# A decoder layer on one core: three raw-weight tiles instead of two, two slots fewer, and four pieces of work issued at other times

## The chip, the cores and the metric

The kernel runs on one core of one Trainium2 chip. The core has a matrix engine (TensorE, PE in the rows; its weight loads are PEld), a vector engine (VectorE, DVE), a scalar engine (ScalarE, ACT), GpSimd (POOL) and a queue engine (SyncE, SP) that here issues the transfers between the chip's main memory and the core's on-chip memory. The metric is the time of one execution on the device, in microseconds (us); lower is better.

## The reference

One inference step of a one-layer decoder, in fp32, width 1024: two half feed-forward layers (FFN, inner width 2816) around a mixing layer of matrix-memory heads (mLSTM) and sliding-window attention (SWA), each between two RMS norms.

```python
def half_ffn(x, j, gpre, gpost):
    y = swiglu(rmsnorm(x, g[gpre]), ffn_w_gate[l, j], ffn_w_up[l, j], ffn_w_down[l, j])
    return x + 0.5 * rmsnorm(y, g[gpost])      # swiglu: (silu(x @ wg) * (x @ wu)) @ wd

x = half_ffn(x, 0, 0, 1)
h = rmsnorm(x, g[2])
...                                            # z = h @ w_in; mLSTM heads and SWA heads on z
u = jnp.concatenate([u_m, u_a], axis=-1)
x = x + rmsnorm(u @ w_out[l], g[3])
x = half_ffn(x, 1, 4, 5)
```

There are 1024 prompt tokens and 8 x 4 sample tokens, 1056 in all.

## The kernel before

**Tiling.** Activations lie with features on the 128 partitions and tokens along the free axis. The 1056 tokens are four quarters q of QW = 264 columns (256 of the prompt, 8 samples). The program has three phases: FFN 1 (phase 1), the mixing layer (phase 2), FFN 2 (phase 3). An fp32 product is made of three matmuls, wh·xh, wh·xl, wl·xh, where h and l are a rounded part and the rest (`mm3` and the loops of the FFN, all recorded at L158).

**Weights.** A raw block of weights, at most 128x1024 fp32 (512 KB), is loaded by SP into one of NRAW tiles called `raw` (`raw_tile`, L217; `prep`, L221). ScalarE casts it in pieces of 512 columns to `wh` and VectorE subtracts `wl = raw - wh` (`split`, L200 and L201). There are NW = 8 tiles each of `wh` and `wl`. A raw tile takes its next load when both have read it. `AHEAD = 3` units are asked for ahead of use.

**FFN.** First the inner activations: for each pair of 128 inner features, TensorE forms sums `gu` by a scheme of seven products from gate and up weights; ScalarE copies some of the sums out of their PSUM bank into `sc` (L957), the activations `h` go to main memory (`store_h`). Then the down projection `pd` in steps of quarters (STEPS): (0,1) and (2,3) in phase 1, (0,1), (2,), (3,) in phase 3. A step loads its `h` back (`load_h`, tiles `hq`, split by the same lines L200 and L201) and runs over 8 output blocks mo of 128 features; a block takes three raw loads (8, 8 and 6 rows of 128x128) and 66 matmuls for each quarter. `out_block` (L634 to L638) scales each result into `y` and sums its squares in `acc`, 528 columns wide: two halves, for the even and the odd mo.

**Norms.** `post` (L556) ends a quarter. `col_stats` adds the two halves of `acc` (VectorE, L248; not in phase 2, where both go to TensorE) and forms column sums `cs` by small matmuls; `rstd` takes the root on VectorE (some ten small instructions, L271 to L280), `row_bcast` spreads it over the partitions on TensorE (`rb`). Then `y*c + x` is formed with `x` loaded back, again with squares and a second `col_stats` for the norm of the next phase. Quarters 0 to 2 of phase 3 end in `store_y` (L1046): transposes of y into a bank `yT` on TensorE, copies `yo` on ScalarE (L1058) or VectorE (L1060), and stores by SP. Quarter 3, the last, is done by the class `Last` (L646), which transposes x and y ahead and block by block.

**What sets the order.** The program is written in the order of a clock `od.now`, TensorE's time as the program estimates it. `od.spawn(generator, delay)` starts side work at a due time, each `yield` moves it on by so many us, and `od.tick` between matmuls lets what is due be written. PQ gives the delay with which `post` starts for each phase and quarter, PW and PL the delays inside it. The tile framework then fixes each engine's order and puts in the waits. All tiles of 528 fp32 columns (x, y, h, hq, sums of activations) come from one pool of NSLOT = 66 slots. PSUM banks of 512 columns are in four groups: 3 "mm", 2 "a", 2 "b", 1 "c" (the statistics).

Of the kernel before, what the change touches and what calls it, by code (L numbers as in the profile page):

```python
# [16 lines left out]
P = 128  # L17
# [6 lines left out]
QW = 264  # L24
# [4 lines left out]
NSLOT, NW, NRAW, NTMP = 66, 8, 2, 8  # L29
# [8 lines left out]
PQ = {1: [4.0, 8.0, 0, 8.0], 2: [2.0, 8.0, 0, 6.0], 3: [0] * 4}  # L38
# [113 lines left out]
def pe(K, out, lhsT, rhs, start=True, stop=True, tr=False, **kw):  # L152
    n = int(np.prod(rhs.shape[1:]))
    if tr:
        K.nc.tensor.transpose(out, lhsT, rhs)
        K.od.now += 0.11
        return
    K.nc.tensor.matmul(out, lhsT, rhs, start=start, stop=stop, **kw)  # L158
    if rhs.dtype == F32R:
        K.od.now += 0.0025 + (n if n >= 213 else 256) / 2400  # L160
    else:
        K.od.now += (4 if rhs.dtype == F32 else 1) * max(n, 64) / 2400
# [79 lines left out]
def col_stats(K, acc, phase):  # L242

    ps = sbank(K, "cs")
    n = 2
    if phase != 2:

        K.nc.vector.tensor_tensor(acc[:, 0:QW], acc[:, 0:QW], acc[:, QW:2 * QW], op=ALU.add)  # L248
        n = 1
    for j, w in enumerate(WIN):  # L250
        for i in range(n):
            pe(K, ps[:, j:j + 1], acc[:, i * QW + w:i * QW + w + P], K.ones, start=(i == 0), stop=(i == n - 1))
    return ps[:, 0:3]
# [302 lines left out]
def post(K, phase, q, y, acc, half, nxt, gpre=None):  # L556

    nc = K.nc
    x = []
    for kp in range(4):  # L560
        t = slot(K, "x")
        nc.sync.dma_start(t, K.xs[q][kp])
        if phase == 1 and q == 0:

            nc.vector.tensor_tensor(pair(t), pair(t), K.r[q].unsqueeze(1).to_broadcast([P, 2, QW]), op=ALU.mult)
        x.append(t)
    yield PW[0]
    ss = col_stats(K, acc.pop(), phase)

    c = rstd(K, ss, 4.0 / D, 4.0 * EPS) if half else rstd(K, ss)  # L570
    yield PW[1]
# [5 lines left out]
    for kp in range(4):  # L577
# [19 lines left out]
        yield PW[2] if q > 1 else PL[phase]  # L597
# [4 lines left out]
    K.od.done.add(("x", phase, q))  # L602
    yield PW[3]
    r = rstd(K, col_stats(K, acc, phase))
# [36 lines left out]
class Last:  # L641
# [30 lines left out]
    def block(self, mo, ps):  # L672
# [16 lines left out]
        if mo == 3:  # L689
            K.od.spawn(self.first(self.t), 3.0)  # L690
        elif mo > 3:
            K.od.spawn(self.second(mo, y), 3.0)
# [197 lines left out]
def ffn(K, phase, j, gpost, nxt, gpre=None):  # L890
# [94 lines left out]
    for si, step in enumerate(steps):  # L985
# [3 lines left out]
        for mo in range(KT):  # L989
# [3 lines left out]
            for q in step:  # L993
                ps[q] = bank(K, "pd", "mm" if last else ("mm", "a", "mm", "b", "mm", "a", "b")[npd % 7])[:, 0:QW]
                npd += 1
# [50 lines left out]
def store_y(K, q, y):  # L1046
    nc = K.nc
    for j in range(3):
        w = P if j < 2 else 8
        for x in range(2):  # L1050
            ps = bank(K, "yT")
# [960 lines left out]
```

## Time and profile before

| | |
|---|---|
| time of three runs | 2021.26 us median (2019.25, 2021.26, 2025.99) |
| profiled execution | 2024.76 us, of which the span of the profile is 2023.0 us |
| instructions in the span | 40250 |
| TensorE | 1982.2 us busy, 98% of the span |
| VectorE, ScalarE | 1168.0 us (58%), 874.9 us (43%) |
| DMA | 216.68 MB, 107 GB/s over the span |
| phase 1: gu, pd | 73 to 483 us, 483 to 749 us |
| phase 3: gu, pd | 1316 to 1726 us, 1726 to 2015 us |

The profile is of one execution, so its stretches add to 2023.0 us; the three runs are other executions of the same program. TensorE is busy nearly everywhere, so what can be had without fewer matmuls is the time in which it waits, and the time in which its clock is not granted in full.

### The profile page before, as it was taken

What the parts mean: (1) busy time and instruction counts of PE and PEld (TensorE: products, weight loads), DVE (VectorE), ACT (ScalarE), POOL (GpSimd) and SP (SyncE); (2) the same over time, 40 slices, a digit from 0 to 9 for tenths busy, and PEclk for the clock granted to TensorE, in tenths of its full rate; (3) what the DMA queues carried; (4) which work ended last, traced back from release to release, by engine and by line L of the source; (5) the groups of instructions that cost most, each with busy time, mean ns of one, the idle gap of its engine ahead of it and who ended that gap; (6) DMA issues with size and microseconds to landing.
All of it is one profiled execution on the core that took longest, in us unless ns stands there. A gap on an engine that the chain in (4) does not pass through costs nothing.

```text
span 2023.0 us, 40250 instructions
## 1 busy us (share of the span) xinstructions
PE 1982.2 (98%) x16108; PEld 1939.7 (96%) x16108; DVE 1168.0 (58%) x2801; ACT 874.9 (43%) x2097; POOL 40.2 (2%) x191
## 2 busy tenths in 40 slices
PE   7999999999999999999999999999999999999997
PEld 6999999999999999987998999999999999999997
DVE  7755555557248336467456758875555556434663
ACT  6533333336346332356253655443333334434553
POOL 1000000000000003000001000000000000000000
PEclk9999999999999999999999999999999999999999
DMA  6223222235356252201324143222223224545773
GB/s 219 70 75 97 74 74 75 87 100 170 95 161 203 89 140 93 53 1 39 97 53 136 43 137 113 107 85 74 75 74 96 74 75 132 155 124 164 223 217 116
DMA packets 281725, 216.68 MB, mean 107 GB/s; under 512 B 21097, under 2 KB 254689, under 8 KB 281537
## 3 DMA queue, kind: packets, MB, share of 16 engines
q1 hardware_dynamic: 281536, 214.11, 35.1%
q8 instruction: 126, 2.06, 0.4%
q14 instruction: 63, 0.51, 0.1%
HBM read 171.38 MB, written 42.49 MB: 106 GB/s over the span
## 4 chain that ended last, share of the span: by engine, by line
PE 87%; DVE 5%; DMA 5%; ACT 2%; issue 1%; SPq 0%; DVEq 0%; ACTq 0%
PE gu L158 40%; PE pd L158 21%; PE pz L158 6%; PE pw L158 4%; PE pl L158 3%; PE pv L158 3%; DMA raw<-ffn_w_down 2%; PE po L158 2%; PE cs L158 1%; DVE wl L201 1%; PE sws L158 1%; PE swo L158 1%; DMA hq<-h 1%; PE E L158 1%; ACT wh L200 1%
## 5 line engine op out<-in xcount | busy, mean ns | idle before, releaser
L158 PE MATMUL gu<-Xl,wh 128*128 128x264 f32 x2240 | 637.4, 285 | 0.0
L158 PE MATMUL gu<-Xh,wh 128*128 128x264 f32 x2240 | 636.6, 284 | 0.3 <-ACT sc L957 0.2
L158 PE MATMUL gu<-Xh,wl 128*128 128x264 f32 x2240 | 635.7, 284 | 0.0
L158 PE MATMUL pd<-hq,wh 128*128 128x264 f32 x2816 | 522.6, 286 | 1.1 <-ACT yo L1058 1.1
L201 DVE TENSOR_TENSOR wl<-raw,wh 128x512 fp32r<-128x512 f32 x450 | 295.9, 668 | 385.0 <-ACT wh L200 379.7
L200 ACT CAST wh<-raw 128x512 fp32r<-128x512 f32 x450 | 265.1, 601 | 457.0 <-PE pd L158 185.7
L158 PEld LDWEIGHTS pd<-hq,wh 128*128 128x128 f32 x2816 | 439.3, 189 | 1.4 <-ACT yo L1058 1.3
L158 PEld LDWEIGHTS gu<-Xh,wl 128*128 128x128 f32 x2240 | 422.3, 189 | 0.0
L158 PEld LDWEIGHTS gu<-Xh,wh 128*128 128x128 f32 x2240 | 421.5, 188 | 0.8 <-ACT sc L957 0.7
L158 PEld LDWEIGHTS gu<-Xl,wh 128*128 128x128 f32 x2240 | 420.8, 188 | 0.0
L158 PE MATMUL pd<-hq,wl 128*128 128x264 f32 x1408 | 402.0, 285 | 0.0
L158 PEld LDWEIGHTS pd<-hq,wl 128*128 128x128 f32 x1408 | 265.9, 189 | 0.0
L957 ACT COPY sc<-gu 128x264 f32<-128x264 f32 x240 | 90.8, 379 | 275.9 <-PE gu L158 273.8
L201 DVE TENSOR_TENSOR wl<-ws,wh 128x512 fp32r<-128x512 f32 x160 | 108.8, 690 | 86.3 <-ACT wh L200 83.3
L968 DVE TENSOR_TENSOR h<-gu,sc 128x264 f32<-128x264 f32 x120 | 51.8, 432 | 105.6 <-PE gu L158 85.4
L158 PE MATMUL pz<-xh,wh 128*128 128x264 f32 x352 | 102.9, 292 | 0.9 <-DVE z L1887 0.9
L158 PE MATMUL pz<-xh,wl 128*128 128x264 f32 x352 | 101.8, 289 | 0.0
L158 PE MATMUL pz<-xl,wh 128*128 128x264 f32 x352 | 101.3, 288 | 0.0
L969 ACT ACTIVATE h<-h 128x264 f32<-128x264 f32 x120 | 50.9, 425 | 106.7 <-DVE h L968 106.7
L200 ACT CAST wh<-ws 128x512 fp32r<-128x512 f32 x160 | 95.8, 623 | 1.5 <-DVE ws L771 1.5
L974 DVE TENSOR_TENSOR sc<-gu,sc 128x264 f32<-128x264 f32 x120 | 51.7, 432 | 56.7 <-PE gu L158 50.9
L158 PE MATMUL pw<-uh,wh 128*128 128x264 f32 x256 | 74.1, 290 | 0.0
(405 smaller groups left out, 2971.2 us busy)
## 6 DMA issues: line engine op xcount, KB each, us to landing
raw<-ffn_w_down SPq DMA_DIRECT2D x80, 512.0 KB
raw<-ffn_w_gate SPq DMA_DIRECT2D x42, 512.0 KB
raw<-ffn_w_up SPq DMA_DIRECT2D x42, 512.0 KB
h<-h SPq DMA_DIRECT2D x80, 264.0 KB
hq<-h SPq DMA_DIRECT2D x160, 132.0 KB
raw<-ffn_w_down SPq DMA_DIRECT2D x40, 384.0 KB
x<-xs SPq DMA_DIRECT2D x48, 264.0 KB
raw<-w_in SPq DMA_DIRECT2D x21, 512.0 KB
```

What stands on the lines that cost most here:

```text
L158: K.nc.tensor.matmul(out, lhsT, rhs, start=start, stop=stop, **kw)
L200: K.nc.scalar.copy(hi, src)
L201: (eng or K.nc.vector).tensor_tensor(lo, src, hi.bitcast(F32), op=ALU.subtract)
L957: nc.scalar.copy(sc[n][:, g], ps)
L968: nc.vector.tensor_tensor(d, bk[tg, g], sc[n][:, g], op=ALU.add)
L969: nc.scalar.activation(d, d, AF.Silu)
L974: nc.vector.tensor_tensor(sc[n][:, g], src, sc[n][:, g], op=ALU.add)
```

## The change

- NRAW goes from 2 to 3: a third raw tile; a load waits for the reads of the third block before it instead of the second. NSLOT goes from 66 to 64.
- The addition of the two halves is taken out of `col_stats` into a new function `halves`, which `post` calls first of all for the first norm, and ahead of the wait PW[3] for the second: 4 and 6 us of `od.now` ahead of the matmuls that read the sum, where it stood right before them.
- In `post`, the four loads of x are issued together; the multiplication of x by its row factor, which only quarter 0 of phase 1 has, moves behind `rstd`.
- In phase 3, `post` starts 3, 7 and 3 us after its step for quarters 0, 1 and 2 (PQ, before 0); quarter 2 steps by PL = 4 us and not PW[2] = 1; the transposes of the first half of the last quarter's y start 5 us after block 3, not 3.
- Banks: the step (2,) of phase 3 takes "mm" for all its `pd` results, as the last step did; `store_y` takes "a" and "b" in turn for quarters 0 and 1 and "b" for quarter 2, where it took "mm".

```diff
--- before.py
+++ after.py
@@ -26,7 +26,7 @@
 
 WIN = [0, 128, 136]
 STEPS = {1: [(0, 1), (2, 3)], 2: [(0, 1), (2, 3)], 3: [(0, 1), (2,), (3,)]}
-NSLOT, NW, NRAW, NTMP = 66, 8, 2, 8
+NSLOT, NW, NRAW, NTMP = 64, 8, 3, 8
 BANKS = dict(mm=3, a=2, b=2, c=1)
 AHEAD = 3
 
@@ -35,7 +35,7 @@
 HW = 0.6
 
 NHELD, NS = 5, 2
-PQ = {1: [4.0, 8.0, 0, 8.0], 2: [2.0, 8.0, 0, 6.0], 3: [0] * 4}
+PQ = {1: [4.0, 8.0, 0, 8.0], 2: [2.0, 8.0, 0, 6.0], 3: [3.0, 7.0, 3.0, 0]}
 XQ = [0, 3.0, 10.0, 20.0]
 PL = {1: 4.0, 2: 2.5, 3: 4.0}
 NP = [1.6, 3.0]
@@ -239,17 +239,20 @@
         K.od.tick()
 
 
-def col_stats(K, acc, phase):
+def halves(K, acc, phase):
+
+    if phase == 2:
+        return [acc[:, 0:QW], acc[:, QW:2 * QW]]
+    K.nc.vector.tensor_tensor(acc[:, 0:QW], acc[:, 0:QW], acc[:, QW:2 * QW], op=ALU.add)
+    return [acc[:, 0:QW]]
+
+
+def col_stats(K, sq):
 
     ps = sbank(K, "cs")
-    n = 2
-    if phase != 2:
-
-        K.nc.vector.tensor_tensor(acc[:, 0:QW], acc[:, 0:QW], acc[:, QW:2 * QW], op=ALU.add)
-        n = 1
     for j, w in enumerate(WIN):
-        for i in range(n):
-            pe(K, ps[:, j:j + 1], acc[:, i * QW + w:i * QW + w + P], K.ones, start=(i == 0), stop=(i == n - 1))
+        for i, s in enumerate(sq):
+            pe(K, ps[:, j:j + 1], s[:, w:w + P], K.ones, start=(i == 0), stop=(i == len(sq) - 1))
     return ps[:, 0:3]
 
 
@@ -556,18 +559,18 @@
 def post(K, phase, q, y, acc, half, nxt, gpre=None):
 
     nc = K.nc
-    x = []
+    sq = halves(K, acc.pop(), phase)
+    x = [slot(K, "x") for _ in range(4)]
     for kp in range(4):
-        t = slot(K, "x")
-        nc.sync.dma_start(t, K.xs[q][kp])
-        if phase == 1 and q == 0:
-
+        nc.sync.dma_start(x[kp], K.xs[q][kp])
+    yield PW[0]
+    ss = col_stats(K, sq)
+
+    c = rstd(K, ss, 4.0 / D, 4.0 * EPS) if half else rstd(K, ss)
+    if phase == 1 and q == 0:
+
+        for t in x:
             nc.vector.tensor_tensor(pair(t), pair(t), K.r[q].unsqueeze(1).to_broadcast([P, 2, QW]), op=ALU.mult)
-        x.append(t)
-    yield PW[0]
-    ss = col_stats(K, acc.pop(), phase)
-
-    c = rstd(K, ss, 4.0 / D, 4.0 * EPS) if half else rstd(K, ss)
     yield PW[1]
     cr = tmp(K, "cr", QW)
     nc.scalar.copy(cr, row_bcast(K, c))
@@ -594,14 +597,15 @@
                 hi, lo = [t[k][g][:, i * QW:(i + 1) * QW] for t in (K.xh, K.xl)]
                 nc.scalar.activation(hi, y[kp][:, s], AF.Copy, scale=gk)
                 nc.vector.scalar_tensor_tensor(lo, y[kp][:, s], gk, hi.bitcast(F32), op0=ALU.mult, op1=ALU.subtract)
-        yield PW[2] if q > 1 else PL[phase]
+        yield PW[2] if q > 1 and phase < 3 else PL[phase]
     if not nxt:
         yield 2.0
         yield from store_y(K, q, y)
         return
     K.od.done.add(("x", phase, q))
+    sq = halves(K, acc, phase)
     yield PW[3]
-    r = rstd(K, col_stats(K, acc, phase))
+    r = rstd(K, col_stats(K, sq))
     yield PW[4]
     if nxt == "mix":
         rc = K.kp.tile([P, 3], F32, tag=f"rc{q}", name=nm(K, "rc"), bufs=1)
@@ -687,7 +691,7 @@
         if mo == 6:
             K.od.spawn(self.stats(0), 2.0)
         if mo == 3:
-            K.od.spawn(self.first(self.t), 3.0)
+            K.od.spawn(self.first(self.t), 5.0)
         elif mo > 3:
             K.od.spawn(self.second(mo, y), 3.0)
 
@@ -991,7 +995,7 @@
                 od.spawn(load_h(K, hs, steps[si + 1]))
             ps = {}
             for q in step:
-                ps[q] = bank(K, "pd", "mm" if last else ("mm", "a", "mm", "b", "mm", "a", "b")[npd % 7])[:, 0:QW]
+                ps[q] = bank(K, "pd", "mm" if len(step) == 1 else ("mm", "a", "mm", "b", "mm", "a", "b")[npd % 7])[:, 0:QW]
                 npd += 1
             for a in range(0, MT, 8):
                 for x, (dh, dl) in enumerate(od.take()):
@@ -1048,7 +1052,7 @@
     for j in range(3):
         w = P if j < 2 else 8
         for x in range(2):
-            ps = bank(K, "yT")
+            ps = bank(K, "yT", "ab"[x] if q < 2 else "b")
             for i in range(4):
                 k = 4 * x + i
                 o = (k % 2) * QW + j * P
```

How the rows of three queues stand before and after, in the order of the program (a name ends in the number of its tile; line numbers behind L158 differ by four between the two programs):

**VectorE, end of step (0,1) of phase 1.** `sq_6408` and `sq_6412` are the squares of quarters 0 and 1, `x` the four loads for quarter 0. Before:

```order
L638 TENSOR_TENSOR sq_6408<-sq_6408,sq_7604 128x528
L565 TENSOR_TENSOR x_7829<-x_7829,rrow_355 128x528
L638 TENSOR_TENSOR sq_6412<-sq_6412,sq_7608 128x528
L201 TENSOR_TENSOR wl_7786<-raw_7783,wh_7785 128x512
L201 TENSOR_TENSOR wl_7790<-raw_7783,wh_7789 128x512
L565 TENSOR_TENSOR x_7832<-x_7832,rrow_355 128x528
L565 TENSOR_TENSOR x_7835<-x_7835,rrow_355 128x528
L565 TENSOR_TENSOR x_7838<-x_7838,rrow_355 128x528
L248 TENSOR_TENSOR sq_6408<-sq_6408 128x264
L201 TENSOR_TENSOR wl_7856<-raw_7853,wh_7855 128x512
L201 TENSOR_TENSOR wl_7860<-raw_7853,wh_7859 128x512
L248 TENSOR_TENSOR sq_6412<-sq_6412 128x264
```

With the change:

```order
L642 TENSOR_TENSOR sq_6408<-sq_6408,sq_7604 128x528
L642 TENSOR_TENSOR sq_6412<-sq_6412,sq_7608 128x528
L201 TENSOR_TENSOR wl_7786<-raw_7783,wh_7785 128x512
L201 TENSOR_TENSOR wl_7790<-raw_7783,wh_7789 128x512
L246 TENSOR_TENSOR sq_6408<-sq_6408 128x264
L201 TENSOR_TENSOR wl_7853<-raw_7850,wh_7852 128x512
L246 TENSOR_TENSOR sq_6412<-sq_6412 128x264
L573 TENSOR_TENSOR x_7830<-x_7830,rrow_355 128x528
L201 TENSOR_TENSOR wl_7857<-raw_7850,wh_7856 128x512
L573 TENSOR_TENSOR x_7831<-x_7831,rrow_355 128x528
L573 TENSOR_TENSOR x_7832<-x_7832,rrow_355 128x528
L573 TENSOR_TENSOR x_7833<-x_7833,rrow_355 128x528
```

The halves of quarter 0 (L248, now L246) are added ahead of the multiplications of x by `rrow`, and those of quarter 1 one row later; all four multiplications stand behind them.

**ScalarE, the change from gu to pd in phase 3.** `hq_...` are activations loaded back, `wh_21569` and `wh_21573` the casts of the first block of down weights, `sc_21605` the copies of the last sums for which TensorE's next `gu` products need the bank. Before:

```order
L200 CAST hq_21517<-hq_21517 128x264
L200 CAST hq_21527<-hq_21527 128x264
L957 COPY sc_21605<-gu_21311 128x264
L200 CAST hq_21531<-hq_21531 128x264
L200 CAST hq_21542<-hq_21542 128x264
L200 CAST hq_21546<-hq_21546 128x264
L957 COPY sc_21605<-gu_21342 128x264
L200 CAST hq_21556<-hq_21556 128x264
L200 CAST hq_21560<-hq_21560 128x264
L200 CAST wh_21569<-raw_21567 128x512
L200 CAST wh_21573<-raw_21567 128x512
```

With the change:

```order
L200 CAST hq_21477<-hq_21477 128x264
L200 CAST wh_21569<-raw_21567 128x512
L200 CAST hq_21481<-hq_21481 128x264
L200 CAST hq_21491<-hq_21491 128x264
L200 CAST hq_21495<-hq_21495 128x264
L200 CAST wh_21573<-raw_21567 128x512
L200 CAST hq_21513<-hq_21513 128x264
L200 CAST hq_21517<-hq_21517 128x264
L200 CAST hq_21527<-hq_21527 128x264
L961 COPY sc_21605<-gu_21311 128x264
L200 CAST hq_21531<-hq_21531 128x264
L961 COPY sc_21605<-gu_21342 128x264
```

The casts of the first down block come ahead of the copies of `sc_21605`; before, they came behind them. SP issues that block's load ahead of the forty `hq` loads, and before it stood among them (behind `hq_21560`); every `hq` load that waits for a slot waits for the matmul for which, before, the second load behind it waited. On TensorE, 12 of the pd matmuls stand among the last 50 gu matmuls. The same rows stand in phase 1.

**SP, end of step (2,) of phase 3.** The raw blocks are those of mo 6 (its third) and mo 7; `o_y` are output stores, `hq` the activations of quarter 3. Before:

```order
L225 DMA raw_23957<-ffn_w_down 128x6x128
L1038 DMA hq_23970<-h_18630 128x264
L1038 DMA hq_23980<-h_18634 128x264
L1038 DMA hq_23990<-h_19116 128x264
L225 DMA raw_24001<-ffn_w_down 128x8x128
L1038 DMA hq_24014<-h_19120 128x264
L1038 DMA hq_24024<-h_19602 128x264
L1038 DMA hq_24034<-h_19606 128x264
L1038 DMA hq_24044<-h_20088 128x264
L225 DMA raw_24051<-ffn_w_down 128x8x128
L1038 DMA hq_24064<-h_20092 128x264
```

With the change:

```order
L225 DMA raw_23961<-ffn_w_down 128x6x128
L1069 DMA o_y_sample<-yo_23797 8x512
L1069 DMA o_y_prompt<-yo_23805 128x512
L1042 DMA hq_23854<-h_16664 128x264
L1069 DMA o_y_sample<-yo_23825 8x512
L1069 DMA o_y_prompt<-yo_23833 128x512
...
L1042 DMA hq_23947<-h_18148 128x264
L1042 DMA hq_23957<-h_18630 128x264
L1042 DMA hq_23977<-h_18634 128x264
L1042 DMA hq_23987<-h_19116 128x264
L1042 DMA hq_23997<-h_19120 128x264
L225 DMA raw_24005<-ffn_w_down 128x8x128
```

Between the last block of mo 6 and the first of mo 7 stand now 18 transfers (6 of them stores, 12 `hq`; eight rows are left out), before 3.

On TensorE, the matmuls `cs` of the second norm stand 6 rows earlier in phase 1 for quarter 0 and 68 rows earlier for quarter 2, which falls in the mixing layer; the `cs` of phase 2's step (0,1) three rows later. The FFN's gate and up loads now have the third block's load ahead of the `store_h` stores; that load waits for a VectorE instruction which comes before those for which the stores wait.

## Rows read from the trace of the kernel before

**Rows 1.** The page of the profile: the span, the engines' busy time (share of the span in brackets, instructions after the x), and the chain of work that ended last.

```profile
span 2023.0 us, 40250 instructions
...
PE 1982.2 (98%) x16108; PEld 1939.7 (96%) x16108; DVE 1168.0 (58%) x2801; ACT 874.9 (43%) x2097; POOL 40.2 (2%) x191
...
PE 87%; DVE 5%; DMA 5%; ACT 2%; issue 1%; SPq 0%; DVEq 0%; ACTq 0%
```

**Rows 2.** Everything that the matmuls of TensorE waited for over the whole span, by line and releaser: us in total, times, the longest (rows of start-up and of small waits left out).

```profile
PE cs L158 <- DVE sq L248: 3.2, 3, 1.7
PE yT L155 <- ACT yo L1058: 2.7, 1, 2.7
...
PE yT L155 <- ACT y L686: 2.2, 2, 1.9
...
PE cs L158 <- DVE sq L587: 1.3, 1, 1.3
...
PE pd L158 <- ACT yo L1058: 1.1, 1, 1.1
PE pz L158 <- DVE z L1887: 0.9, 1, 0.9
...
PE yT L155 <- DVE y L579: 0.8, 1, 0.8
...
PE cs L158 <- DVE sq L638: 0.6, 1, 0.6
...
PE gu L158 <- ACT sc L957: 0.2, 1, 0.2
```

**Rows 3.** VectorE's instructions in order of time about 620 us (start, busy us, line, operation, out and in, count): the end of the first half of phase 1's down projection.

```profile
619.42 1.29 DVE L201 TENSOR_TENSOR wl<-raw,wh 128x512 fp32r<-128x512 f32 x2
620.63 1.94 DVE L565 TENSOR_TENSOR x<-x,rrow 128x528 f32<-128x528 f32 x3
622.48 0.43 DVE L248 TENSOR_TENSOR sq<-sq 128x264 f32<-128x264 f32 x1
```

**Rows 4.** Stretches of 2 us at four places where TensorE had waited: busy time and instructions of PE, PEld, DVE, ACT and POOL, then PEclk, the granted clock of TensorE as a share of full speed, DMA share and GB/s.

```profile
623.00:625.00 2.00, 1.94 (x14) 1.97 (x15) 1.86 (x5) 0.60 (x2) 0.00 (x0) 0.87 0.97 324
625.00:627.00 2.00, 2.00 (x11) 2.00 (x10) 1.15 (x8) 0.44 (x1) 0.00 (x0) 0.50 0.78 216
627.00:629.00 2.00, 2.00 (x15) 2.00 (x15) 0.91 (x2) 0.58 (x2) 0.00 (x0) 0.78 0.30 88
...
786.00:788.00 2.00, 2.00 (x11) 2.00 (x11) 0.97 (x5) 0.00 (x0) 0.19 (x1) 0.50 0.86 266
...
1894.00:1896.00 2.00, 2.00 (x12) 2.00 (x11) 1.48 (x3) 0.95 (x2) 0.00 (x0) 0.56 0.94 281
1896.00:1898.00 2.00, 2.00 (x12) 2.00 (x12) 1.00 (x2) 1.93 (x5) 0.00 (x0) 0.59 0.98 299
...
1938.00:1940.00 2.00, 1.98 (x16) 1.98 (x17) 0.41 (x1) 1.06 (x2) 0.00 (x0) 1.00 0.99 347
```

**Rows 5.** Stretches of 10 us in the two last steps of phase 3, with the columns of rows 4.

```profile
1886.00:1896.00 10.00, 7.32 (x55) 7.08 (x55) 5.20 (x9) 5.13 (x10) 0.00 (x0) 0.91 0.63 188
...
1936.00:1946.00 10.00, 9.00 (x75) 8.79 (x74) 6.10 (x18) 3.86 (x10) 0.00 (x0) 1.00 0.72 224
1946.00:1956.00 10.00, 8.84 (x74) 8.39 (x73) 9.19 (x16) 5.83 (x14) 0.00 (x0) 1.00 0.57 166
1956.00:1966.00 10.00, 9.75 (x82) 9.11 (x80) 4.59 (x9) 4.92 (x10) 0.00 (x0) 1.00 0.73 215
1966.00:1976.00 10.00, 9.06 (x74) 9.06 (x75) 4.30 (x8) 4.46 (x11) 0.00 (x0) 1.00 0.62 183
1976.00:1986.00 10.00, 7.57 (x62) 7.12 (x62) 4.65 (x8) 6.10 (x13) 0.00 (x0) 1.00 0.50 148
```

**Rows 6.** The chain that ended last, of 1926 to 1992 us alone: its shares by line, and one of its eight transfers.

```profile
by line: DMA raw<-ffn_w_down 53.5%; PE pd L158 11.4%; issue 10.3%; ACT wh L200 9.1%; DVE wl L201 8.9%; DVE y L579 1.5%; PE yT L155 1.5%; DVE yo L1060 1.0%; DVE y L578 0.9%; ACT yT L712 0.7%; ACT hq L200 0.5%; ACT y L634 0.4%; ACTq L200 0.3%
...
1927.92 4.61 DMA raw<-ffn_w_down
```

**Rows 7.** All casts of raw down-projection weights on ScalarE, 1926 to 1992 us: duration in ns (least, median, most), the first and the last start, forms.

```profile
L200 ACT CAST wh<-raw x42: 400/618/623, 1926.2 to 1991.4; 128x512 fp32r<-128x512 f32 x35, 128x256 fp32r<-128x256 f32 x7
```

**Rows 8.** The subtractions that follow those casts on VectorE, and all DMA traffic of 1926 to 1990 us.

```profile
L201 DVE TENSOR_TENSOR wl<-raw,wh 128x512 fp32r<-128x512 f32 (+1 forms) x40 | 24.3, 642 | 28.3 <-ACT wh L200 26.5 <-PE pd L158 1.3
...
DMA packets 20942, 12.97 MB, mean 203 GB/s; under 512 B 528, under 2 KB 19385, under 8 KB 20937
```

**Rows 9.** TensorE's gu matmuls of 1714 us, in order of time (between the two rows shown stand 45 others, one matmul each).

```profile
1713.77 0.28 PE L158 MATMUL gu<-Xh,wh 128*128 128x264 f32 x1
...
1719.40 0.29 PE L158 MATMUL gu<-Xl,wh 128*128 128x264 f32 x1
```

**Rows 10.** ScalarE about the first change from gu to pd, the DMA issues of SP about the second (SPq; the duration is that of the whole run of issues), and ScalarE there.

```profile
475.93 0.79 ACT L200 CAST hq<-hq 128x264 fp32r<-128x264 f32 x2 [0.16 <-DMA hq<-h]
476.63 0.37 ACT L957 COPY sc<-gu 128x264 f32<-128x264 f32 x1
...
1706.16 12.94 SPq L1038 DMA_DIRECT2D hq<-h  x26
...
1718.99 1.10 ACT L200 CAST hq<-hq 128x264 fp32r<-128x264 f32 x3 [0.82 <-DMA hq<-h]
1720.00 0.37 ACT L957 COPY sc<-gu 128x264 f32<-128x264 f32 x1
```

## The prediction

> **What bounds the kernel now.** I read the page first. TensorE is busy 98% of 2023.0 us and 87% of the chain that ended last is TensorE [rows 1]; the change takes no matmul away, so it can only win back waits of TensorE and stretches in which its clock is not granted in full. Second view: what its matmuls waited for [rows 2]. The sums `cs` wait for the addition of the halves (L248) three times, 3.2 us in all; other waits hang on transposed outputs (`yo`, `y`). The gu stretches, where most of the work lies, wait 0.2 us.
>
> Third view: the granted clock after a wait. From 623 to 629 us it was 0.87, 0.50 and 0.78 in three stretches of 2 us, at 1894 us 0.56 and 0.59 [rows 4]. The missing shares times 2 us give 0.85 x 2 = 1.7 us at both places; 0.50 of full speed is the lower of the two levels. It fell to 0.50 behind the wait of 783 us too, but stayed at 1.00 behind that of 1937 us [rows 4]. So a wait costs its length, and sometimes 1.7 us on top.
>
> Last view: the two last steps of phase 3. From 1936 to 1986 us TensorE was busy 9.00 + 8.84 + 9.75 + 9.06 + 7.57 = 44.2 of 50 us, from 1886 to 1896 us 7.32 of 10 [rows 5]. In this stretch the chain is not TensorE's: 53.5% are loads of raw down weights, 11.4% pd matmuls [rows 6]. The 42 casts of 1926.2 to 1991.4 us belong to 21 blocks [rows 7], 65.2/20.5 = 3.2 us a block, 9.5 us for the three of an output block. TensorE needs less: 46 matmuls took 5.63 us, 0.122 us each [rows 9], so 66 take 8.1 us, with the eight transposes of a block, at the same pitch, 9.0. Raw supply, with two tiles, bounds it here.
>
> **The change part by part.**
>
> *Third raw tile, end of phase 3.* A tile's cycle is two of the intervals, 6.4 us: a load (4.6 us in the one shown [rows 6]), two casts at 0.62 us [rows 7], the last subtraction (0.64 us, [rows 8]), some of it overlapped. With three tiles the same cycle gives a block every 2.1 us and 6.4 us per output block, under the 8.1 to 9 that TensorE needs. The cover of the loads is then TensorE itself. The lost time is 50 - 44.2 = 5.8 us after 1936 us and 2.7 us at 1890 us, with 1.7 us of clock behind it. The 2.7 us wait is for `yo` [rows 2]: copies that stand on ScalarE behind a cast whose block is late. With the supply ahead and `store_y` on banks of its own, I expect all of it back: 10.2 us. Not all may come: the transposes of the last quarter share one "b" bank pair with `store_y` and need an eviction between neighbours (512 columns, as the cast's 0.62 us [rows 7]), and 18 transfers now stand ahead of the first block of mo 7. At 0.50 us an issue (12.94/26, [rows 10]) these are 9 us, against two output blocks (16 us) before the block is needed. The bound is from 0 to 3.5 us (a wait of 1.8 and a clock fall of 1.7); I take 0.8, nearest to single evictions.
>
> *Halves earlier.* At 621 us `cs` waits 1.7 us, the longest of its three [rows 2], as VectorE works three multiplications (1.94 us) and then the addition, 622.48 to 622.91 [rows 3]. Now the addition stands right behind the subtraction that ends at 620.71, so it is ready about 621.1, and TensorE asked 1.7 us ahead of 622.91, at 621.2 or a little later. Back come 1.7 us and the clock's 1.7: 3.4 us. The other two share 3.2 - 1.7 = 1.5 us. That of 1937 us is the 1.0 missing in the first of the five stretches [rows 5] and already in the 5.8; that of 656 us, 0.5, goes likewise: 0.5. The added instructions are none; the multiplications moved behind `rstd` are VectorE work beside pd matmuls.
>
> *Quarter 2's second norm, in the mixing layer.* Its `cs` stand 68 rows earlier on TensorE, so the pieces that crowd the wait `pz <- z` (0.9 us, [rows 2]) spread out. That wait may go or stay, and with it the clock: 0 to 0.9 + 1.7 = 2.6 us. I take most of the wait, 0.7, and half of the clock's 1.7, since behind another wait of about this length, that of 1937 us, it did not fall [rows 4]: 1.6.
>
> *Phase 2's step.* `cs` is asked three matmuls later, 0.4 of the 0.6 us [rows 2]. The wait for L587 (1.3 us) stays.
>
> *Two slots fewer, and the down block's load ahead.* At each change from gu to pd, `hq` loads take slots that gu matmuls free, and each now waits for the matmul of the second load behind it: two loads at 0.50 us [rows 10], 1.0 us later. ScalarE, which was waiting for those loads (0.82 us), also casts the first down block there, two casts, before the copy of `sc`; 1.24 - 0.82 = 0.4 us more, partly overlapped, say 0.2. Queued behind are the copies at 1720.00 and 476.63 us [rows 10], for which gu needs the bank. In phase 3 TensorE already waited 0.2 us for this copy [rows 2], so the delay shows: 1.1 us after one pd matmul that is moved into it. In phase 1 it did not, so some 0.4 us is cover: 0.7. Together 1.8 us lost, bounds 0 and 1.8 + 2 x 1.7 = 5.2 if the clock falls both times. The pd matmuls moved among gu cost nothing of their own.
>
> *Issued later, and nothing else.* The later start of `post` in phase 3, its slower pace for quarter 2 and the later transposes of the last quarter move small matmuls and transposes to other places among pd matmuls of the same steps, with the same count; their cover is the 64.5 us of a step (8 x 66 x 0.122 [rows 9]). If it were gone, by running past the end of step (2,), each pair of `yT` would be a wait of about 0.62 us in the last step; that is in the 3.5 above. The stores that `store_y` issues move with it and are the 18 transfers counted there. The four x loads of a `post` are issued in one piece, 4 x 0.50 us of SP's queue [rows 10], with a raw block ahead of them where there was one behind: no pd wait for `wh` or `wl` appears among TensorE's waits [rows 2], so that is hidden by blocks already split. In gu the third block is issued ahead of the `h` stores but waits for an earlier VectorE instruction than they do; that VectorE work hides it. Bounds: the gu wait of 0.2 us from below, and see the third rival.
>
> Sum: 10.2 - 0.8 + 3.4 + 0.5 + 1.6 + 0.4 - 1.8 = **13.5 us** shorter. Against the profiled execution's 2024.76 us that is 2011.3; that execution lies 3.5 us above the median of the runs, 2021.26, so the runs should come at about **2008 us**.
>
> **A rule against it.** The loads of 1926 to 1990 us moved 203 GB/s [rows 8], while stretches of 2 us reached 347 GB/s at a DMA share of 0.99 [rows 4]; so there is room. The Trainium skill, "DMA: Bandwidth & Descriptors", § Issuing engines are not separate DMA queues, states that all transfers run on the same 16 DMA engines and interleave there, so another one in flight adds no bandwidth of itself. By that rule alone a third load only stretches the other two; it is the first rival, and the trace agrees with it only where the share is near 0.99.
>
> **Rivals.**
>
> *1. The loads share, and supply stays the bound.* If a load in flight with two others takes 3/2 of its time, a block still comes every 3.2 us and the 5.8 us stay lost; the wait of 1890 us too. Against it speak shares of 0.50 to 0.73 over the 50 us [rows 5]; for it, the 18 transfers in one run and the stretches near 0.99. Then 13.5 - 9.4 = 4.1 us remain: about 2017 us.
>
> *2. The halves come no earlier in time.* If VectorE is behind when `halves` is due, the waits at 621, 656 and 1937 us stay with the clock's fall: 3.4 + 0.5 + 1.0, and the mixing layer's 1.6 with them, 6.5 us less: about 2014 us. For it: VectorE runs without a break before 622 us [rows 3]. Against it: its order has the addition ahead of what delayed it.
>
> *3. Slower: SP's queue in gu.* SP issues in order. If the third block's load, now ahead of four `h` stores, waits at the queue's head, the stores are late, and slots, two fewer, come free late for the next pair's `h`. This would come with each pair of inner blocks that stores, 10 in each FFN, 20 in all; from 13.5/20 = 0.7 us a pair on it eats the whole gain, and at 1.1 us a pair it ends 8.5 us slower, about 2030 us. Against it speaks the order of the waits; for it, that ScalarE's copies already touch TensorE there (0.2 us).
>
> **How the numbers follow.** Forecast 0.66 (2004 to 2012 us: with every gain in full and no loss 10.2 + 3.4 + 0.5 + 2.6 + 0.6 = 17.3 us, 2004; with the losses at their bounds 13.5 - 2.7 - 3.4 = 7.4 us, 2014). Rival 1: 0.14, rival 2: 0.10, rival 3: 0.06, the rest for none of these. A measurement of this kernel tells about 0.3%, 6 us, from no change: below 2015.2 us is faster, so forecast and rival 2 count as faster (0.77 with a part of the rest), rival 1 as the same (0.14), rival 3 as slower (0.09). The range goes 3 us below 2004, as the runs of before spread by 6.7 us, and up to rival 1 and a little beyond: 2001 to 2018 us.
>
> **What would show it.** No `cs` wait for the halves at 621, 656 and near 1930 us, and a clock of 1.00 behind the first; the chain from 1910 us on made of pd matmuls, casts spaced evenly by 2.7 to 3.0 us, TensorE busy 10 of 10 us; a new wait of about 1 us of gu for `sc` just ahead of each pd. Wrong would be: casts still 3.2 us apart, a wait of pd for `wh` or `wl` in mo 7 of the step (2,), gu waiting in every pair, or clock falls at new places: each costs 1.7 us.

## The result, and the profile after

The changed kernel takes 2006.36 us (median of five runs, 2005.70 to 2009.42) against 2021.26 us, 14.9 us less. Against runs of the kernel before on the same chip the ratio is 0.9929, 95% interval 0.9910 to 0.9948, which is 14.4 us. The forecast was 2008 us and 13.5 us less. The profiled execution is that of 2009.42 us; its page, in the columns of [rows 1]:

```profile
span 2007.5 us, 40282 instructions
...
PE 1975.5 (98%) x16108; PEld 1934.2 (96%) x16108; DVE 1168.1 (58%) x2801; ACT 873.2 (43%) x2097; POOL 40.0 (2%) x191
```

What TensorE waited for, as [rows 2]. Of the three waits for the halves none is left, nor those for `yo`, `y` and `z`. New are `gu <- sc`, 3.1 us instead of 0.2, and 0.9 for a sum of VectorE at the same place:

```profile
PE gu L158 <- ACT sc L961: 3.1, 2, 2.2
...
PE sinter L158 <- DMA Cb<-state_mlstm_C: 1.2, 1, 1.2
...
PE xT L155 <- ACT xT L673: 1.1, 1, 1.1
PE gu L158 <- DVE sc L978: 0.9, 1, 0.9
...
PE rb L155 <- DVE v L274: 0.7, 1, 0.7
...
PE cs L158 <- DVE sq L590: 0.4, 1, 0.4
```

The last steps, in the columns of [rows 5] and at the same times, where the work is up to 15 us further on:

```profile
1886.00:1896.00 10.00, 10.00 (x88) 9.91 (x87) 5.96 (x10) 5.33 (x12) 0.00 (x0) 1.00 0.81 247
1936.00:1946.00 10.00, 9.83 (x83) 9.62 (x81) 7.81 (x13) 6.35 (x14) 0.00 (x0) 1.00 0.70 199
1946.00:1956.00 10.00, 9.12 (x76) 9.12 (x77) 7.38 (x13) 7.14 (x16) 0.00 (x0) 1.00 0.67 188
1956.00:1966.00 10.00, 10.00 (x86) 10.00 (x86) 6.11 (x11) 5.89 (x12) 0.00 (x0) 1.00 0.76 229
1966.00:1976.00 10.00, 10.00 (x85) 9.68 (x84) 5.15 (x9) 6.36 (x12) 0.00 (x0) 1.00 0.62 183
1976.00:1986.00 10.00, 10.00 (x85) 10.00 (x84) 4.79 (x9) 4.79 (x9) 0.00 (x0) 1.00 0.38 114
```

From 1936 to 1986 us TensorE is busy 48.95 of 50 us, before 44.2; the one gap left is a wait of 1.1 us for the copy of `xT`. The chain of the stretch with the same work as in [rows 6], here 1910 to 1976 us, and its casts, as [rows 7]:

```profile
by line: PE pd L158 81.7%; PE yT L155 6.6%; PE xT L155 3.6%; issue 1.6%; DVE y L582 1.1%; ACT wh L200 1.0%; DVE y L581 1.0%; ACT xT L673 0.9%; PE cs L158 0.9%; DVE wl L201 0.5%; PE rb L155 0.5%; ACT sq L685 0.4%; ACT y L690 0.3%; DVEq L201 
...
L200 ACT CAST wh<-raw x46: 401/620/647, 1912.5 to 1975.0; 128x512 fp32r<-128x512 f32 x39, 128x256 fp32r<-128x256 f32 x7
```

Before, 53.5% of the chain were loads and 11.4% pd; now 81.7% are pd. 46 casts are 23 blocks, (1975.0 - 1912.5)/22.5 = 2.8 us each instead of 3.2. That is TensorE's own pace: 8.1 to 9.0 us for the three blocks of an output block, by the prediction's count from [rows 9].

Cut at the first `gu` of phase 1, the first `pz` of the mixing layer, the first `gu` of phase 3 and the last matmul, the profiled executions divide as follows (us). The second column's bracket is the clock not granted in it: the sum of (1 - PEclk) x 2 over all its stretches of 2 us. In phases 1 and 3 it was 1.7 and 1.7 before, 3.4 and 5.1 in e1, 3.4 and 0 in e2, and 0 in the others of the table.

| kernel | phase 1 | mixing (clock) | phase 3 |
|---|---|---|---|
| before | 676.0 | 566.9 (8.5) | 698.3 |
| changed | 674.6 | 562.5 (6.8) | 688.1 |
| changed, another execution | 673.3 | 556.1 (0) | 687.1 |
| third tile alone (e2) | 679.8 | 558.9 (1.7) | 686.6 |
| change with two tiles (e1) | 677.5 | 562.1 (5.1) | 705.3 |
| change, halves late (e3) | 675.4 | 559.3 (1.7) | 687.1 |
| change, phase 3 times and banks as before (e4; again) | 673.2; 674.4 | 563.5 (8.5); 557.7 (0) | 686.2; 687.2 |

### The profile page after: what moved, and what is told of

It is laid out like the page before. It is cut to its first block, busy times and chain, and to the rows that moved or that the text cites. A ratio compares the mean times of both kernels' runs of the same rounds, so it can differ in the third digit from the quotient of the medians.

```text
span 2007.5 us, 40282 instructions
## 1 busy us (share of the span) xinstructions
PE 1975.5 (98%) x16108; PEld 1934.2 (96%) x16108; DVE 1168.1 (58%) x2801; ACT 873.2 (43%) x2097; POOL 40.0 (2%) x191
## 4 chain that ended last, share of the span: by engine, by line
PE 92%; DVE 3%; ACT 2%; DMA 2%; issue 0%; SPq 0%; DVEq 0%; ACTq 0%
PE gu L158 40%; PE pd L158 25%; PE pz L158 7%; PE pw L158 5%; PE pl L158 3%; PE pv L158 2%; PE po L158 2%; ACT sws L1330 1%; PE cs L158 1%; PE swo L158 1%; PE E L158 1%; PE yT L155 1%; PE sws L158 1%; DMA hq<-h 1%; PE S L158 0%
## 5 line engine op out<-in xcount | busy, mean ns | idle before, releaser
L158 PE MATMUL gu<-Xh,wh 128*128 128x264 f32 x2240 | 636.5, 284 | 4.0 <-ACT sc L961 3.1
L158 PE MATMUL gu<-Xl,wh 128*128 128x264 f32 x2240 | 636.9, 284 | 0.0
L158 PE MATMUL gu<-Xh,wl 128*128 128x264 f32 x2240 | 635.8, 284 | 0.0
L158 PE MATMUL pd<-hq,wh 128*128 128x264 f32 x2816 | 521.1, 286 | 0.0
L158 PEld LDWEIGHTS pd<-hq,wh 128*128 128x128 f32 x2816 | 437.1, 189 | 0.1
L158 PEld LDWEIGHTS gu<-Xh,wh 128*128 128x128 f32 x2240 | 421.6, 188 | 4.7 <-ACT sc L961 3.5
L158 PEld LDWEIGHTS gu<-Xh,wl 128*128 128x128 f32 x2240 | 421.6, 188 | 0.0
L158 PEld LDWEIGHTS gu<-Xl,wh 128*128 128x128 f32 x2240 | 421.1, 188 | 0.0
L158 PE MATMUL pd<-hq,wl 128*128 128x264 f32 x1408 | 400.4, 284 | 0.0
L158 PEld LDWEIGHTS pd<-hq,wl 128*128 128x128 f32 x1408 | 264.8, 188 | 0.0
L158 PE MATMUL pz<-xh,wh 128*128 128x264 f32 x352 | 102.3, 291 | 0.0
L158 PE MATMUL pz<-xh,wl 128*128 128x264 f32 x352 | 101.1, 287 | 0.0
L158 PE MATMUL pz<-xl,wh 128*128 128x264 f32 x352 | 100.7, 286 | 0.0
L158 PE MATMUL pw<-uh,wh 128*128 128x264 f32 x256 | 73.8, 288 | 0.0
```

## The experiments

"Measured" is the ratio to the kernel before, run beside it, with its 95% interval.

**What carries the last steps.** Three kernels. The first (e1) takes the third tile out of the change:

```diff
-NSLOT, NW, NRAW, NTMP = 64, 8, 3, 8
+NSLOT, NW, NRAW, NTMP = 66, 8, 2, 8
```

> The changed kernel with two raw tiles and 66 slots again; the earlier halves and the later issue and other banks of phase 3 stay. Theory (the third tile carries the last steps): the casts of 1920 to 1990 us stay about 3.2 us apart and TensorE loses 5 us or more there; the changes from gu to pd lose nothing (0.2 us of waiting for sc, as before); the halves keep their 3.4 + 0.5 + 2.5 us. Together 6 to 9 us under the kernel before, 2012 to 2015 us. Rival (timings and banks carry the last steps): the last steps lose under 2 us, and with the gu to pd waits gone it is at or under the changed kernel, 2002 to 2006 us.

Measured: 1.0023 (1.0006 to 1.0041), a little slower than the kernel before, which neither side expected. Its waits, and two stretches of its last steps:

```profile
PE rb L155 <- DVE v L274: 3.9, 2, 2.9
PE yT L155 <- DVE yo L1064: 3.9, 2, 3.1
PE yT L155 <- ACT yo L1062: 3.6, 3, 1.5
...
PE pd L158 <- ACT wh L200: 2.7, 2, 1.5
...
1916.00:1926.00 10.00, 8.12 (x53) 7.48 (x52) 6.22 (x14) 6.38 (x17) 0.00 (x0) 0.87 0.98 296
...
1976.00:1986.00 10.00, 5.29 (x38) 4.84 (x39) 5.76 (x10) 5.45 (x12) 0.00 (x0) 0.94 0.75 226
```

With two tiles the loads are 45.6% of the chain from 1900 to 1990 us. The later issue with its banks made it worse: the transposes of quarter 2 and the first of quarter 3 share the two "b" banks, their evictions `yo` stand on ScalarE and VectorE behind casts and subtractions of blocks that are late, and TensorE waits for both in turn, 4.7 of 10 us from 1976 us on. Phase 3 is 7 us longer than before; 3.4 of these are clock not granted (5.1 against 1.7). The second kernel (e2) is the opposite, only the first line of the diff:

> The kernel before with three raw tiles and 64 slots, nothing else. Theory: the last steps give back 6 to 9 us of their 10 (output transposes and pd still share banks), the two changes from gu to pd cost 3 to 4 us, the waits for the halves at 621 and 656 us stay: 3 to 6 us under the kernel before, 2015 to 2018 us. Rival (timings and banks carry the last steps): only the loss at gu to pd is left, 2021 to 2025 us.

Measured: 0.9954 (0.9939 to 0.9969), 9 us, more than the theory's 3 to 6. All waits in the last steps but one of 0.5 us (the last row) are gone, and phase 3 is 11.7 us shorter; the other rows show what the other parts are for:

```profile
PE cs L158 <- DVE sq L248: 3.2, 2, 2.3
PE gu L158 <- ACT sc L957: 2.8, 2, 1.5
...
PE cs L158 <- ACT sq L681: 0.5, 1, 0.5
PE cs L158 <- DVE sq L587: 0.4, 1, 0.4
```

That line of the diff also takes two slots away; by themselves these change nothing (e5 below, 0.9997), so it is the tile.

The third (e4) puts the times and banks of phase 3 back, with three tiles (PQ, PW for quarter 2, `first` at 3.0, `pd` and `yT` banks; the first line is shortened):

```diff
-PQ = {... 3: [3.0, 7.0, 3.0, 0]}
+PQ = {... 3: [0] * 4}
...
-        yield PW[2] if q > 1 and phase < 3 else PL[phase]
+        yield PW[2] if q > 1 else PL[phase]
...
-            K.od.spawn(self.first(self.t), 5.0)
+            K.od.spawn(self.first(self.t), 3.0)
...
-                ps[q] = bank(K, "pd", "mm" if len(step) == 1 else ("mm", "a", "mm", "b", "mm", "a", "b")[npd % 7])[:, 0:QW]
+                ps[q] = bank(K, "pd", "mm" if last else ("mm", "a", "mm", "b", "mm", "a", "b")[npd % 7])[:, 0:QW]
...
-            ps = bank(K, "yT", "ab"[x] if q < 2 else "b")
+            ps = bank(K, "yT")
```

> The changed kernel with the times and banks of phase 3 as before (PQ, PW for quarter 2, the first transposes of the last quarter, pd and yT banks). Theory (the third tile carries the last steps): 1 to 4 us above the changed kernel, as copies of yT again hold banks that pd needs, 2007 to 2010 us; casts evenly spaced under 3 us. Rival (timings and banks carry them): 8 to 11 us above, 2014 to 2017 us.

Measured: 0.9924 (0.9901 to 0.9947), and in another set of runs:

> The changed kernel with the times and banks of phase 3 as before, once more. Theory (they are worth nothing with three tiles): within 2 us of the changed kernel, 0.991 to 0.994. Rival: 0.995 or more.

0.9930 (0.9913 to 0.9947). Beside 0.9929 and 0.9928 of the changed kernel that is no difference; its phase 3 is 686.2 and 687.2 us against 688.1 and 687.1. Both sides of the first expectation took the later issue to be worth 1 us or more. With three tiles it is worth nothing that these runs can tell; with two, phase 3 is 8.4 us longer with it (705.3 against 696.9 in e6 below), of which 3.4 are clock not granted. What e4 has beyond e2 is the part in `post` alone: 0.9924 against 0.9954 in the same set of runs, about 6 us. So of some 14 us the tile is worth about 9 and the part in `post` most of the rest.

**The halves.** The additions of both norms back in their old place, x still multiplied behind the root (e3):

```diff
-    sq = halves(K, acc.pop(), phase)
-    ss = col_stats(K, sq)
+    ss = col_stats(K, halves(K, acc.pop(), phase))
...
-    sq = halves(K, acc, phase)
     yield PW[3]
-    r = rstd(K, col_stats(K, sq))
+    r = rstd(K, col_stats(K, halves(K, acc, phase)))
```

> The changed kernel with the halves added right before the sums again; the multiplications of x stay behind the root. Theory (the early addition is what removes the waits): cs waits of 0.4 us or more for the halves come back at two or three of 621, 656 and 1930 us and the wait of z near 783 us with its clock fall, 3 to 7 us above the changed kernel, 2009 to 2013 us. Rival (moving the four multiplications of x away is enough at 621 us, and the rest is small): 0 to 2 us above, 2006 to 2008 us.

Measured: 0.9932 (0.9909 to 0.9956), the rival's number. The waits come back only in part: none at 621 us, 1.4 at 656 us, 0.9 for `z` (with no fall of the clock behind it), none in the last steps:

```profile
PE cs L158 <- DVE sq L246: 1.4, 1, 1.4
...
PE pz L158 <- DVE z L1889: 0.9, 1, 0.9
...
PE rb L155 <- DVE v L274: 0.5, 1, 0.5
```

These two are 2.3 us together, and they seem not to be free: with the clock taken off, these four executions take 2.2 us more than the changed kernel's (table in the next section; standard error about 1). The ratio doesn't show it, since their clock happened to be granted better.

The other half of that pair (e10): x multiplied early again, halves early.

> The changed kernel with the multiplications of x ahead of the first norm's sums again, as before, and the halves early. Theory of the prediction (the early addition removes the wait at 621 us): no cs wait over 0.3 us there, and within 1.5 us of the changed kernel. Rival (the multiplications are what delayed VectorE, and the late halves cost nothing once they are gone): a wait of 1 us or more for the second quarter's sums or for rb between 620 and 640 us, with or without a clock fall, 2 to 5 us above the changed kernel.

Measured: 0.9926 (0.9907 to 0.9945), again no difference from the changed kernel. There is no `cs` wait at 621 us; 1.5 us of waiting come as `rb`, for the root:

```profile
PE gu L158 <- ACT sc L961: 2.1, 2, 1.2
...
PE rb L155 <- DVE v L274: 1.5, 1, 1.5
```

That looks like the rival's sign, but it doesn't tell the two apart: e4 run once more, which has both edits, also waits 1.5 us for `rb` at 628 us. So, with three tiles, either edit alone takes the wait at 621 us away: moving the addition ahead of the multiplications, or the multiplications away. Phase 1 is 674.9 us here, 675.4 with the halves late, 673.3 and 674.6 with both, and 679.8 with neither (e2; 3.4 of it clock not granted). The part in `post` alone, on two tiles (e6):

> The kernel before with the part in post alone: halves ahead of their sums, x loads together, x multiplied behind the root. Theory (these waits are TensorE's own): 3 to 7 us under the kernel before, 0.9965 to 0.9985, with no cs wait for the halves in phase 1 and no wait of z. Rival (with two raw tiles the wait moves on to rb, which the root is late for, as in the run with two tiles and all the rest): rb waits 2 us or more near 628 us with its clock fall, and the gain is 0 to 2 us.

Measured: 0.9980 (0.9965 to 0.9995), 4 us, inside the theory's range, and its signs came: no `cs` wait in phase 1, none of `z`. Phase 1 is 2.2 us shorter than before. A part of its waits is passed on to `rb`, 1.0 us each at 627 and 659 us with no fall of the clock. The last steps keep theirs; the `cs` wait below is there, at 1930 us, and is longer than before (2.0 against 1.0), so what removes that one is the third tile and not the early halves:

```profile
PE yT L155 <- ACT yo L1062: 2.3, 1, 2.3
...
PE rb L155 <- DVE v L274: 2.0, 2, 1.0
PE cs L158 <- DVE sq L246: 2.0, 1, 2.0
```

**The wait for `sc`.** First the two slots alone (NSLOT 64, two tiles; e5):

> The kernel before with 64 slots, nothing else. Theory (two slots fewer make the loads of h late and with them the copies of sc): gu waits 0.5 to 1.5 us for sc at one or both changes to pd, 0.5 to 3 us above the kernel before. Rival (the casts of the first down block ahead of the copies do it, which two raw tiles don't allow): gu waits for sc 0.3 us or less in all, and no change beyond the noise.

Measured: 0.9997 (0.9981 to 1.0013). No wait for `sc`; one of 1.3 us at 483 us for the first down block. Its load stands behind 32 `hq` loads, as before; counted from the first `gu` it was issued 0.4 us later, and its cast began 7.1 us after the issue instead of 5.6:

```profile
PE cs L158 <- DVE sq L248: 3.9, 3, 2.5
...
PE pd L158 <- ACT wh L200: 1.3, 1, 1.3
```

Then 66 slots with three tiles, room for which seven `wh` and `wl` tiles make (NW = 7; phase 3 timed as before; e7):

> The changed kernel with the times and banks of phase 3 as before, seven tiles each of wh and wl instead of eight, and the 66 slots that this gives room for. Theory (slots make the copies of sc late): gu waits for sc fall from 2 to 3 us to under 1 us, 1 to 3 us under the changed kernel. Rival (eight split pieces are needed as cover): pd or gu wait for wh or wl, 0 to 5 us above the changed kernel.

Measured: 1.0044 (1.0028 to 1.0059). The products `pl` that begin phase 1 end 12 us later (first `gu` at 85.7 us, else 72 to 74). TensorE stands still for 7.7 us up to 59 us, for a bank that ScalarE reads only at 58.6 us, behind casts of activations that wait for VectorE; from 73 us on ScalarE waits 6.9 and 2.7 us for TensorE to give a `wh` tile back, which it doesn't in e4. Why seven tiles lead to that order is not shown.

```profile
PE pl L158 <- ACT h L889: 7.7, 1, 7.7
...
PE gu L158 <- ACT sc L961: 2.0, 2, 1.3
```

With 66 slots the waits for `sc` are still 2.0 us. So two slots fewer neither make the wait (e5) nor are needed for it (e7, which has seven split tiles besides). The order doesn't make all of it either: e6, with two tiles and 66 slots, waits 0.8 us at 1713 us for a copy that stands behind a late `hq` load. Last, the copies of `sc` given precedence in the last pair, in the changed kernel (e8b) and in the one with the times of phase 3 as before (e8):

```diff
-                        nc.scalar.copy(sc[n][:, g], ps)
+                        if mat and p == MT // 2 - 1:
+                            with K.tc.high_priority():
+                                nc.scalar.copy(sc[n][:, g], ps)
+                        else:
+                            nc.scalar.copy(sc[n][:, g], ps)
```

> The changed kernel, with the copies of the last sums (sc) given precedence over ScalarE's other work in the last pair before pd: they stand three casts earlier in its order. Theory (the casts of hq and of the first down block ahead of the copies make them late): gu waits for sc fall from about 2.7 us to under 1 us, 1 to 3 us under the changed kernel, a ratio to the kernel before of 0.9910 to 0.9925. Rival (ScalarE is late as a whole, since 64 slots make the loads late): the wait moves to pd, which waits for wh or hq 1 us or more, and the ratio stays at 0.993.

> The same precedence for the copies, with the times and banks of phase 3 as before the change. Theory (third tile carries the last steps, the later issue is worth nothing with it): at or 0 to 2 us under the run with the copies first alone, a ratio of 0.990 to 0.9925; no wait for xT or yT in the last steps. Rival (the later issue helps, the earlier measurement of it was chance): 2 us or more above that run.

Measured: 0.9926 (0.9910 to 0.9942) and 0.9918 (0.9898 to 0.9938). In the first the wait for ScalarE's copies is gone, and at the same places 1.3 us of waiting for VectorE's sums are left. In the second, where the copy also stands three casts earlier, 1.2 us of waiting for it are left and 1.6 for VectorE's sums, 2.8 in all; the two profiles of e4, without the precedence, have 2.2 and 3.1. The rows of the first, then of the second:

```profile
PE gu L158 <- DVE sc L982: 1.3, 3, 0.5
...
PE pd L158 <- ACT wh L200: 0.6, 1, 0.6
...
PE gu L158 <- DVE sc L982: 1.6, 3, 0.6
...
PE gu L158 <- ACT sc L963: 1.2, 1, 1.2
```

The wait of 0.6 us for `wh` is not at these places: it is at 1910 us, in mo 7 of the step (2,), and the next section comes back to it.

The second has the lowest ratio of all, but its interval holds those of the changed kernel, so nothing here is shown to beat it. Last of all the changed kernel itself once more (a1, "another execution"):

> The changed kernel once more, beside the others of this call. Both theories: a ratio to the kernel before of 0.991 to 0.995. The clock falls near 1100 us (6.8 us in the first profile) are another number, 0 to 6.8 us, if they are chance and not of the program.

Measured: 0.9928 (0.9909 to 0.9948). The clock not granted near 1100 us was 0, against 6.8 in the first profile; the last section has its rows.

## Why the prediction was right

**The sum and its parts.** 13.5 us were forecast, 14.4 to 14.9 measured. *Third tile, last steps*: 9.4 net forecast (10.2 - 0.8). From the first matmul of pd alone to the end it is 1727.6 to 2014.6 us before (ten matmuls taken off the start, which the change moved forward: the trace has ten among the last gu, not 12) and 1723.7 to 1999.1 us after, 287.0 and 275.4 us: 11.6. Of these 7.5 are waits (9.0 us of idle TensorE before, 1.5 after) and 1.7 clock; the other 2.4 are neither, and the runs don't say where they lie. The bound was raw supply, as read from the chain, and e1, e2, e4 and e5 show that the tile alone lifts it. The 0.8 for `store_y`'s bank and the 18 transfers was near the 1.05 us of the one wait, for a copy of `xT` on the "b" bank (0.3 in the other execution). No block of mo 7 is waited for here, but in e8b, which issues phase 3 in the same way, its second block is, 0.6 us for `wh` and 0.2 for `wl`: the sign that the prediction named, in one of the five profiles with this issue (e10 has 0.2 there).

*Halves, phase 1*: 3.9 forecast; phase 1 is 1.4 us shorter although it holds 1.8 us of the new wait, so 3.2; in the other execution 2.7 + 1.5 = 4.2. The first has a new wait of 0.7 us for the root (`rb`), which the step left out. The mechanism was half right: the step named the three multiplications ahead of the addition and counted on the addition's place, but e3 shows that moving the multiplications away is enough at 621 us. The early addition takes away the 1.4 us at 656 us (e3, whose phase 1 is 0.8 to 2.1 us longer) and the wait of `z`.

*Mixing layer*: 1.6 + 0.4 forecast. The waits of 783 and 1257 us are gone with both clock falls, 0.9 + 0.6 + 3.4, and the wait for L587, which I had left at 1.3, fell to 0.4. The wait of `z` at 783 us is the early halves': it is gone in e1 and e6 and stays in e2 and e3. The other two are the third tile's: e2 has 0 and 0.4, e6 has 0.4 and 1.3, and `cs` stands three matmuls later in e2 too. Without the clock the layer takes 566.9 - 8.5 = 558.4 us before and 555.7 after, 2.7 less; the waits named make 2.4 of it.

*The step that failed* is "Two slots fewer, and the down block's load ahead". It was sized 1.8 us and put down to loads made late by slots (1.0 at each change) with the casts as a small rest (0.4, of which 0.2 was counted). Measured were 0.90 + 0.94 in phase 1 and 2.21 - 0.2 in phase 3, 3.9 us, and 2.5 in the other execution. ScalarE of the changed kernel there, and TensorE:

```profile
1713.24 0.62 ACT L200 CAST wh<-raw 128x512 fp32r<-128x512 f32 x1
1713.76 1.03 ACT L200 CAST hq<-hq 128x264 fp32r<-128x264 f32 x3
1714.70 0.61 ACT L200 CAST wh<-raw 128x512 fp32r<-128x512 f32 x1
1715.22 1.03 ACT L200 CAST hq<-hq 128x264 fp32r<-128x264 f32 x3
1716.16 0.36 ACT L961 COPY sc<-gu 128x264 f32<-128x264 f32 x1
...
1714.09 0.28 PE L158 MATMUL pd<-hq,wh 128*128 128x264 f32 x1
1716.58 0.40 PE L158 MATMUL gu<-Xh,wh 128*128 128x264 f32 x1 [2.21 <-ACT sc L961]
```

ScalarE runs without a break from 1713.24 us: two casts of the first down block stand among the `hq` casts, and behind them comes the copy at 1716.16 us. Its sum had ended over 1.5 us earlier: TensorE's last product before the wait is the pd at 1714.09 us, and only sums ahead of that can be copied. The two casts take 1.04 us of ScalarE there (to the start of the next, 0.52 each), where 0.2 was counted. So the failed part is the cause given: with three tiles the wait comes with 64 slots (e2, 2.8 us) and with 66 (e7, 2.0), and with two tiles and 64 slots it doesn't come (e5). That ScalarE's order is what makes it fits e8b, where the wait for the copies went, but e8 kept 1.2 us of it with the same precedence; how much is order and how much ScalarE being late as a whole stays open. No fall of the clock followed any of these waits.

**The rivals.** *Loads that share*: with three tiles 1910 to 1974 us moved 245 GB/s against 203 before [rows 8], while TensorE waited less. The shares of 0.50 to 0.73 before [rows 5] left room. By the Trainium skill, "DMA: Bandwidth & Descriptors", § Issuing engines are not separate DMA queues, such transfers run on the same 16 DMA engines and interleave, whichever engine issues them. The trace agrees where these are full: 1920 to 1930 us moved 313 GB/s at a share of 1.02, no more than the 347 at 0.99 before [rows 4]. *Halves no earlier*: no `cs` wait for the halves is left. *SP in gu*: gu waits nowhere but in the last pair.

**The place of the numbers.** That the sum agrees with the median so closely is in part luck. Of its 13.5 us, 1.7 + 1.7 + 0.85 = 4.25 were clock, read behind three waits of one profile, and whether the clock falls behind such a wait is chance: in e5 nothing fell behind 2.5 us of waiting at 624 us, in e6 nothing behind 2.3 us at 1885 us. Each execution on record has its span and its mean granted clock; their product estimates the time with the clock taken off, the rest of the span is the clock not granted. Means over all executions, in us:

| kernel | executions | span x clock | clock not granted |
|---|---|---|---|
| before | 55 | 2007.3 | 10.4 |
| changed | 10 | 1995.8 | 8.4 |
| third tile alone (e2) | 7 | 1999.2 | 9.8 |
| part in `post` alone (e6) | 12 | 2005.8 | 9.2 |
| change with two tiles (e1) | 10 | 2009.3 | 12.1 |
| change, halves late (e3) | 4 | 1998.0 | 6.5 |
| change, x early (e10) | 6 | 1996.0 | 6.0 |
| change, phase 3 as before (e4, both) | 10 | 1995.0 | 8.0 |

The standard error of a mean is 0.3 to 1.0 us in the third column and 0.5 to 2.6 in the last. So the work is 11.5 us shorter, where 13.5 - 4.25 = 9.25 were forecast, and the clock gave about 2 us, where 4.25 were: two misses that cancel. Within the work, the last steps gave more than forecast and the copies of `sc` cost more. The part in `post` is worth 1.5 us on two tiles and 4.2 on three (e2 to e4).

## What to carry to other kernels

When the chain of a stretch is made of loads though the engine is nearly 90% busy, divide a tile's cycle by the number of tiles and compare it with the consumer's pace: here a load, two casts and a subtraction are 4.6 + 1.2 + 0.6 = 6.4 us, so 6.4/2 = 3.2 against 2.8 us a block. One more tile was worth more than all the rearranging of small work, and the rearranging in `post` was worth more behind it. Rearranging around a starved queue can even cost (e1): in-order engines then hold evictions behind casts that wait. And work that is ready earlier goes earlier into every in-order queue: look at what stands behind it there.

## What the runs showed of the hardware

The clock of TensorE, when it falls, goes to 0.50, the lower of its two levels, and the missing clock comes in steps of 1.7 us. Whether it falls behind a given wait differs between executions of one program. Near 1100 us all kernels wait 1.1 to 2.1 us for a state load. The first profile of the changed kernel, and then that of the other execution of the same program, a few us behind that wait (columns of [rows 4]):

```profile
1102.00:1104.00 2.00, 2.00 (x11) 2.00 (x11) 0.60 (x3) 0.54 (x1) 0.27 (x2) 0.50 0.80 241
...
1108.00:1110.00 2.00, 2.00 (x14) 1.77 (x11) 1.74 (x6) 0.00 (x0) 0.19 (x1) 0.50 0.30 82
...
1100.00:1102.00 2.00, 2.00 (x30) 1.28 (x30) 1.76 (x5) 1.98 (x3) 0.00 (x0) 1.00 0.77 237
...
1106.00:1108.00 2.00, 2.00 (x22) 1.47 (x21) 0.51 (x1) 1.14 (x4) 0.00 (x0) 1.00 0.07 16
```

In the first, the clock is at 0.50 from 1100.5 to 1114 us: 6.8 us missing, four times 1.7 without a break. In the second, none is missing. In the two profiles of e4 it was 6.8 and 0 us too; over the 14 profiles it was 0 in four, 1.7 in four, 3.4 and 5.1 in one each, and 6.8 in four. This one place makes up most of the difference between executions of the changed kernel (2009.42 us with 6.8, 1999.54 us with 0), and half of the change's worth. Nor does the length of a wait by itself decide: 2.2 us at 1714 us were followed by no fall, 0.6 us at 1257 us before the change were. A single pair of spans can't measure 0.3% (6 us) here. Segments with the clock taken off repeat better, to 0.4 to 2.7 us between two executions of one program (the changed kernel and e4), and so do the products of span and clock: over ten executions of the changed kernel they scatter by 1.3 us (standard deviation), the spans by 2.9.
